# A hybrid decoder block on one core: the split weights of even and odd channel tiles are laid half a block and 128 bytes apart

## The chip, the cores and the metric

One of the eight cores of a Trainium2 chip runs the whole layer. The metric is the device time in microseconds of one execution; the kernel before took 1539.01 us (median of 3 runs, 1537.67 to 1539.15).

## The reference

The input is 256 tokens of width 2048; 16 learned meta tokens are put in front, which makes 272. All numbers are float32.

```
xn   = rms(h, n1);  proj = xn @ w_in                # 2048 x 10704
z_rwkv, z_fox, z_gate = split(proj)
y_a  = rwkv7(lerp of z_rwkv with the token before)  # 16 heads of 64, recurrence over tokens
y_b  = fox(z_fox)                                   # 16 heads, causal softmax with forget gates
merged = sigmoid(z_gate_a) * (y_a @ w_a) + sigmoid(z_gate_b) * (y_b @ w_b)
h    = h + merged @ w_o
gate, up = split(rms(h, n2) @ w_gate_up)            # 2048 x 2 x 5632
out  = h + (silu(gate) * up) @ w_down               # 5632 x 2048; the meta tokens are dropped
```

## The kernel before

Every large product is done with split operands. A float32 weight block `raw` of 128 partitions by 1024 columns is loaded by a DMA from SyncE's queue; ScalarE rounds it into `wh` (type float32r, the high part), VectorE subtracts and leaves `wl` (the low part). This is `wload` (L304). Activations are held as such pairs too: `xhl` (the normed input), `hts` (the FFN's input), `yas` and `ybs` (the branches) have the shape [128, channel tile, 2, 272], so high and low part of one channel tile lie side by side and one channel tile comes 2 x 272 = 544 columns (2176 bytes) after the other. A product is then high x high + high x low + low x high, all float32r, added up in PSUM.

A weight block of 1024 columns is `kb` channel tiles of `cols` columns each: two of 512 in the FFN (`gt`, `up`), w_o and w_down; four of 256 in the products of w_in and in the branches (`br`). In the kernel before they lie one behind the other, so the channel tiles of a block start 2048 or 1024 bytes apart.

`cm_jobs` (L432) makes products with the weights stationary and the tokens moving. For each of the block's `nm` output tiles of 128 columns and each channel tile it either calls `mm2` (L418: one matmul of 512 columns, high weights against both parts of 256 tokens, then one of 256 columns with the low weights) or `mm3` (L346 to 349: three matmuls of n columns: high weights and high tokens, high weights and low tokens, low weights and high tokens). n is 272 for k, v of RWKV and k, v of fox, 258 for RWKV's r, 256 for the branches; `mm2` serves the gates `zg`, fox's q (`f` with 512 columns), `gt` and `up`. Each matmul is preceded by a load of its 128x128 stationary tile (LDWEIGHTS), which the profile lists as PEld and which overlaps the matmul ahead of it.

`tm_jobs` (L1286) serves w_o (`wo`) and w_down (`dn`): there the activations (`mgh`, `mgl`, `ach`, `acl`; step 1024 bytes from one channel tile to the next) are stationary and the weights move, 512 columns in two rows of 256. `wload` is called with `gap=True` for it and puts each row of 256 columns behind 16 free ones, in steps of 272. Its three matmuls are L1304 (high activations, high weights), L1305 (low, high), L1306 (high, low).

The order of the work on TensorE is written out by hand (`manual_schedule`): `run` loads a block, does the multiplications of the block before, and so on; between matmuls `slot` (L386) lets in the small steps of the RWKV recurrence and of the attention when their due time has come. The other engines are put in order by a planner. Weights have four buffers each for `raw`, `wh` and `wl` in a pool at the low end of SBUF, ahead of `xhl` and `hts`. In this layout all weight buffers begin 128 bytes past a multiple of 256, and so do `xhl` and `hts`; `yas`, `ybs`, `mgh`, `mgl`, `ach`, `acl` begin 224 bytes past one.

In the RWKV recurrence `XT` (a transposed 32x32 block for each of 8 chunks and 2 heads) and `QT` are two tiles of 128 x 8 x 32. XT is written by VectorE, 16 matmuls read one half of its rows, ScalarE copies their result into the other half of the rows of QT (L962), and 16 matmuls read that.

Of the kernel before, what the change touches and what calls it, by code (L numbers as in the profile page):

```python
# [9 lines left out]
F32 = mybir.dt.float32  # L10
# [8 lines left out]
P = 128  # L19
D = 2048  # L20
NMETA = 16

T = 256
L = NMETA + T
# [10 lines left out]
KT = D // P  # L35
# [17 lines left out]
EB = 8  # L53
GATEB = 3
PSM = 4
WCOLS = 4 * L

LANES = 112
BETWEEN = 2
# [41 lines left out]
def hybrid_block(ctx, tc, A, out, dbg=None):  # L101
    nc = tc.nc
# [31 lines left out]
    for h in range(2):  # L134
        rows = slice(h * HD, (h + 1) * HD)
# [50 lines left out]
    rw = rw_pool.__enter__()  # L186
# [114 lines left out]
        nc.tensor.matmul(pz, zw, zw, start=True, stop=True)  # L301


    def wload(parts, n, between=None, gap=False):  # L304

        raw = wp.tile([P, 1024], F32, tag="raw", name="raw", bufs=RAWB)
        wh = wp.tile([P, WCOLS], F32R, tag="wh", name="wh", bufs=WB)
        wl = wp.tile([P, WCOLS], F32R, tag="wl", name="wl", bufs=WB)  # L310
        if gap:

            (_, _, shape, ((_, src),)), = parts
            nc.sync.dma_start(raw.rearrange("p (k c) -> p k c", c=shape[1]), src)
            rr = raw.rearrange("p (r c) -> p r c", c=T)
            th, tl = (t.rearrange("p (r c) -> p r c", c=L)[:, :, NMETA:] for t in (wh, wl))
            nc.scalar.activation(th, rr, AF.Copy)  # L317
            nc.vector.tensor_tensor(tl, rr, th.bitcast(F32), op=ALU.subtract)  # L318
            return [(th, tl)]
        res = []  # L320
        for prow, c0, shape, srcs in parts:
            size = 1
            for d in shape:
                size *= d
            names = " ".join(f"d{i}" for i in range(len(shape)))
            kw = {f"d{i}": d for i, d in enumerate(shape)}

            def v(t):
                return t[:prow, c0:c0 + size].rearrange(f"p ({names}) -> p {names}", **kw)

            for sel, src in srcs:
                nc.sync.dma_start(v(raw)[sel], src)
            if between is not None:
                between(len(res))
            cs_ = slice(c0, c0 + size)
            nc.scalar.activation(wh[:prow, cs_], raw[:prow, cs_], AF.Copy)  # L336
            nc.vector.tensor_tensor(wl[:prow, cs_], raw[:prow, cs_], wh[:prow, cs_].bitcast(F32), op=ALU.subtract)  # L337
            res.append((v(wh), v(wl)))
        return res

    ALL = slice(None)

    def kblock(ap):
        return ap.rearrange("(k p) c -> p k c", p=P)

    def mm3(ps, wh, wl, ah, al, first, last):  # L346
        nc.tensor.matmul(ps, wh, ah, start=first, stop=False)  # L347
        nc.tensor.matmul(ps, wh, al, start=False, stop=False)  # L348
        nc.tensor.matmul(ps, wl, ah, start=False, stop=last)  # L349
# [58 lines left out]
    def run(jobs):  # L408
        for load, mul in jobs:
            w = load()  # L410
            finish_job()
            pending.append(lambda w=w, mul=mul: mul(w))
# [6 lines left out]
    def mm2(ps, wh, wl, act, first, last):  # L419

        if last:
            nc.tensor.matmul(ps[:, :T], wl, act[:, 0, :], start=False, stop=False)
        nc.tensor.matmul(ps.rearrange("p (a t) -> p a t", a=2), wh, act, start=first, stop=last)  # L423
        if not last:
            nc.tensor.matmul(ps[:, :T], wl, act[:, 0, :], start=False, stop=False)  # L425
# [3 lines left out]
        nc.scalar.activation(dst, ps[:, :T], AF.Copy)  # L429
        nc.vector.tensor_tensor(dst, dst, ps[:, T:], op=ALU.add)  # L430

    def cm_jobs(wap, nk, act, n0, n, post, alloc=main_ps, name="cm", two=True):  # L432


        box = []
        cols = wap.shape[1]
        nm, kb = cols // P, 1024 // cols

        def mk(q):
            def load():  # L440
                return wload([(P, 0, [kb, cols], [((ALL,), kblock(wap[q * kb * P:(q + 1) * kb * P, :]))])], 1024)

            def mul(w):
                (wh, wl), = w
                if q == 0:
                    box.extend(alloc(f"{name}_{m}") for m in range(nm))
                for m in range(nm):
                    ms = slice(m * P, (m + 1) * P)
                    for k in range(kb):
                        kt = q * kb + k  # L450
                        a = act[:, kt, :, n0:n0 + n]
                        if n == T and two:
                            mm2(box[m], wh[:, k, ms], wl[:, k, ms], a, kt == 0, kt == nk - 1)
                        else:
                            mm3(box[m][:, :n], wh[:, k, ms], wl[:, k, ms], a[:, 0], a[:, 1], kt == 0, kt == nk - 1)
                        slot(3 * n / 2.4)
                if q == nk // kb - 1:
                    post(box)
            return load, mul
        return [mk(q) for q in range(nk // kb)]  # L460
# [47 lines left out]
    def lora_jobs():  # L508
        box = []

        def mk(q):
            def load():
                raw = raw0 if q == 0 else wp.tile([P, 1024], F32, tag="raw", name="raw", bufs=RAWB)
                wh = wp.tile([P, WCOLS], F32R, tag="wh", name="wh", bufs=WB)
                wl = wp.tile([P, WCOLS], F32R, tag="wl", name="wl", bufs=WB)
                if q > 0:
# [197 lines left out]
    def rwkv_bg(g, box):  # L714
        kr, vr, rr, sg_, ag, gg = (box[n] for n in ("k", "v", "r", "sig", "aa", "gg"))
        rr = rr[:, :, :T]
# [55 lines left out]
        parts = [et(f"{n}{g}").bitcast(F32R)[:, :, :T] for n in ("rkh", "rkl")]  # L772
# [98 lines left out]
        for s_ in range(31):  # L871
            n, w = s_ // 3 + 1, 31 - s_
# [6 lines left out]
        for j in range(3):  # L879
            n = 11 if j < 2 else 10  # L880
# [68 lines left out]
        meta_steps = step(-1, S, BK0, SV0, NK0, X0, None)  # L949

        XT = rw.tile([P, 8, 32], F32, tag="xt", name=f"XT{g}", bufs=1)
        QT = rw.tile([P, 8, 32], F32, tag="qt", name=f"QT{g}", bufs=1)
        nc.vector.transpose(XT, X[:, :, 0:32])
        next(meta_steps)
        yield Y_XT, ("chain", 2)
        ps = aux_ps(f"QT{g}")
        up, dn = (lambda h: slice(h * HD, h * HD + 32)), (lambda h: slice(h * HD + 32, h * HD + HD))
# [36 lines left out]
        for cc in range(2):  # L994
            for h in range(2):
                dst = yg[hb(h)].rearrange("p m (e f t) -> p m e f t", f=2, t=HD)[:, :, :, cc, :]
                src = ps[hb(cc), :].rearrange("p (m e h t) -> p m e h t", m=2, e=2, h=2)[:, :, :, h, :]
# [189 lines left out]
    gt = None  # L1187
# [36 lines left out]
    gt = gt_pool.__enter__()  # L1224
# [55 lines left out]
    hts = hp.tile([P, KT, 2, L], F32R, tag="hts", name="hts")  # L1280
# [4 lines left out]
    def tm_jobs(wap, nk, ah, al, post, name):  # L1285

        box = []

        def mk(q):
            def load():  # L1290
                return wload([(P, 0, [2, 512], [((ALL,), kblock(wap[q * 256:(q + 1) * 256, :]))])], 1024, gap=True)

            def mul(w):
                (wh, wl), = w
                if q == 0:
                    box.extend(main_ps(f"{name}_{t}") for t in range(2))
                end = q == nk // 2 - 1
                for k, t in ((0, 0), (1, 0), (0, 1), (1, 1)):
                    kt = q * 2 + k
                    ts_ = slice(t * P, (t + 1) * P)  # L1300
                    first, last = kt == 0, kt == nk - 1
                    o = box[t].rearrange("p (a c) -> p a c", a=2)
                    hi, lo_ = wh[:, 2 * k:2 * k + 2], wl[:, 2 * k:2 * k + 2]
                    nc.tensor.matmul(o, ah[:, kt, ts_], hi, start=first, stop=False)  # L1304
                    nc.tensor.matmul(o, al[:, kt, ts_], hi, start=False, stop=False)  # L1305
                    nc.tensor.matmul(o, ah[:, kt, ts_], lo_, start=False, stop=last)  # L1306
                    if end and k == 1:
                        post(t, box[t])
            return load, mul
        return [mk(q) for q in range(nk // 2)]  # L1310
# [41 lines left out]
    wgu = A["w_gate_up"][0]  # L1352
    for j in range(DFF // 512):
        gs = [hp.tile([P, T], F32, tag="ga", name=f"ga{j}{m}", bufs=8) for m in range(4)]

        def post_gate(pss, gs=gs):
            for g, ps in zip(gs, pss):
                halves(g, ps)
                nc.vector.tensor_tensor(g, g, rsb2, op=ALU.mult)
                nc.scalar.activation(g, g, AF.Silu)  # L1360

        def post_up(pss, gs=gs, j=j):
            for m, (g, ps) in enumerate(zip(gs, pss)):
                ub = hp.tile([P, T], F32, tag="ub", name=f"ub{j}{m}", bufs=2)
                halves(ub, ps)
                nc.vector.tensor_tensor(ub, ub, rsb2, op=ALU.mult)
                nc.vector.tensor_tensor(ub, ub, g, op=ALU.mult)
                split(ach[:, 4 * j + m, :], acl[:, 4 * j + m, :], ub)
        run(cm_jobs(wgu[:, j * 512:(j + 1) * 512], KT, hts, NMETA, T, post_gate, name=f"gt{j}"))
        run(cm_jobs(wgu[:, DFF + j * 512:DFF + (j + 1) * 512], KT, hts, NMETA, T, post_up, alloc=aux_ps, name=f"up{j}"))  # L1370
    wdn = A["w_down"][0]
    for j in range(4):
# [70 lines left out]
```

## Time and profile before

| | |
|---|---|
| median of 3 runs | 1539.01 us (1537.67 to 1539.15) |
| the profiled execution | 1540.85 us |
| its span in the trace | 1539.1 us |
| PE busy | 1529.6 us (99%), 10113 matmul records |
| PE weight loads busy | 1352.5 us (88%) |
| VectorE, ScalarE, GpSimd busy | 1030.4, 778.2, 106.8 us |
| DMA | 283.32 MB, mean 184 GB/s |

The span runs from the first to the last instruction of the profiled execution. The length that is recorded for one matmul is longer than the time to the start of the next, as matmuls overlap; what the engine needs for one is seen in the distance of the starts. By time, the products of w_in with the recurrence and the attention run to about 613 us, the branches to 705, w_o to 797, `gt` and `up` to 1291 and w_down to the end.

### The profile page before, as it was taken

Reading aid. Unit: us, or ns where it says so; the run is one execution under the profiler, and the core shown is the slowest. Engines: PE = TensorE matmul, PEld = TensorE weight load, DVE = VectorE, ACT = ScalarE, POOL = GpSimd, SP = SyncE. Lnnn points to the kernel's source line nnn. Section 1 sums busy time; section 2 is a strip of 40 time slices with the busy share of each in tenths; the row PEclk is TensorE's granted clock in tenths of the full one; section 3 lists DMA queues with packets and bytes.
Section 4 is the critical chain, followed back from the end, with each engine's and each line's share of the span. In section 5 each row is a group of like instructions: output and inputs, shape, how many; then the busy total and the mean of one; then the engine's idle time right before and its main releaser. Section 6 shows DMA issues by size and latency. Waiting matters only on the chain.

```text
span 1539.1 us, 25987 instructions
## 1 busy us (share of the span) xinstructions
PE 1529.6 (99%) x10113; PEld 1352.5 (88%) x10113; DVE 1030.4 (67%) x1859; ACT 778.2 (51%) x1174; POOL 106.8 (7%) x186
## 2 busy tenths in 40 slices
PE   9999999999999999999999999999999999999998
PEld 9999899989989888998888888888888888888887
DVE  7887698688788857876565566666556666444443
ACT  7654465475465445554455455445445544333332
POOL 2111203302202000000000000000000000000000
PEclk9999999999999999999999999999999999999999
DMA  8566546546645757777566666666666665566663
GB/s 269 163 171 185 148 134 188 163 119 188 175 125 154 212 155 218 230 226 240 181 180 185 192 185 186 191 192 182 189 191 191 182 190 189 191 204 204 189 203 104
DMA packets 211483, 283.32 MB, mean 184 GB/s; under 512 B 23888, under 2 KB 128352, under 8 KB 211360
## 3 DMA queue, kind: packets, MB, share of 16 engines
q1 hardware_dynamic: 206752, 277.53, 60.7%
q10 hardware_dynamic: 4608, 4.13, 0.8%
q8 instruction: 79, 1.29, 0.3%
q14 instruction: 44, 0.36, 0.1%
HBM read 274.43 MB, written 7.19 MB: 183 GB/s over the span
## 4 chain that ended last, share of the span: by engine, by line
PE 95%; DVE 2%; ACT 1%; DMA 1%; SPq 1%; issue 1%; DVEq 0%; ACTq 0%
PE up L423 11%; PE gt L423 10%; PE zg L423 8%; PE dn L1306 5%; PE dn L1305 5%; PE dn L1304 5%; PE up L425 5%; PE gt L425 5%; PE zg L425 4%; PE f L347 2%; PE f L349 2%; PE f L348 2%; PE br L347 2%; PE f L423 2%; PE br L348 2%; PE br L349 2%
## 5 line engine op out<-in xcount | busy, mean ns | idle before, releaser
L337 DVE TENSOR_TENSOR wl<-raw,wh 128x1024 fp32r<-128x1024 f32 (+1 forms) x376 | 456.7, 1216 | 264.0 <-ACT wh L336 263.4
L336 ACT ACTIVATE wh<-raw 128x1024 fp32r<-128x1024 f32 (+1 forms) x376 | 393.9, 1049 | 424.8 <-PE up L423 117.5
L318 DVE TENSOR_TENSOR wl<-raw,wh 128x1024 fp32r<-128x1024 f32 x120 | 147.0, 1225 | 162.8 <-ACT wh L317 162.7
L423 PE MATMUL gt<-hts,wh 128*128 128x512 f32 x704 | 245.0, 394 | 0.0
L423 PE MATMUL up<-hts,wh 128*128 128x512 f32 x704 | 244.9, 394 | 0.0
L317 ACT ACTIVATE wh<-raw 128x1024 fp32r<-128x1024 f32 x120 | 127.0, 1058 | 194.4 <-PE dn L1305 141.5
L425 PE MATMUL gt<-hts,wl 128*128 128x256 f32 x660 | 186.2, 282 | 0.0
L425 PE MATMUL up<-hts,wl 128*128 128x256 f32 x660 | 186.0, 282 | 0.0
L423 PE MATMUL zg<-xhl,wh 128*128 128x512 f32 x512 | 182.4, 401 | 0.0
L423 PEld LDWEIGHTS up<-hts,wh 128*128 128x128 f32 x704 | 130.1, 188 | 26.5
L423 PEld LDWEIGHTS gt<-hts,wh 128*128 128x128 f32 x704 | 130.1, 188 | 26.5
L1305 PE MATMUL dn<-wh,acl 128*128 128x512 f32 x352 | 138.7, 394 | 0.0
L1306 PE MATMUL dn<-wl,ach 128*128 128x512 f32 x352 | 138.3, 393 | 0.0
L1304 PE MATMUL dn<-wh,ach 128*128 128x512 f32 x352 | 138.1, 392 | 0.0
L425 PE MATMUL zg<-xhl,wl 128*128 128x256 f32 x480 | 135.0, 281 | 0.0
L425 PEld LDWEIGHTS up<-hts,wl 128*128 128x128 f32 x660 | 124.7, 189 | 1.8
L425 PEld LDWEIGHTS gt<-hts,wl 128*128 128x128 f32 x660 | 124.7, 189 | 1.8
L423 PEld LDWEIGHTS zg<-xhl,wh 128*128 128x128 f32 x512 | 94.3, 188 | 19.4 <-issue 0.7
L425 PEld LDWEIGHTS zg<-xhl,wl 128*128 128x128 f32 x480 | 90.6, 189 | 1.2
L1304 PEld LDWEIGHTS dn<-wh,ach 128*128 128x128 f32 x352 | 66.0, 188 | 15.7
L1305 PEld LDWEIGHTS dn<-wh,acl 128*128 128x128 f32 x352 | 66.1, 188 | 15.4
L1306 PEld LDWEIGHTS dn<-wl,ach 128*128 128x128 f32 x352 | 66.1, 188 | 14.7
(464 smaller groups left out, 2937.9 us busy)
## 6 DMA issues: line engine op xcount, KB each, us to landing
raw<-in_w_gate_up_dram SPq DMA_DIRECT2D x176, 512.0 KB, 3.7
raw<-in_w_in_dram SPq DMA_DIRECT2D x160, 512.0 KB, 4.1
raw<-in_w_down_dram SPq DMA_DIRECT2D x88, 512.0 KB, 4.8
raw<-in_w_o_dram SPq DMA_DIRECT2D x32, 512.0 KB, 4.1
raw<-in_w_branch_a_dram SPq DMA_DIRECT2D x16, 512.0 KB, 4.6
raw<-in_w_branch_b_dram SPq DMA_DIRECT2D x16, 512.0 KB, 4.7
zgd<-zg ACTq DMA_DIRECT2D x30, 128.0 KB, 1.7
gate<-zgd SPq DMA_DIRECT2D x15, 256.0 KB, 6.0
```

The source lines that it names most:

```text
L317: nc.scalar.activation(th, rr, AF.Copy)
L318: nc.vector.tensor_tensor(tl, rr, th.bitcast(F32), op=ALU.subtract)
L336: nc.scalar.activation(wh[:prow, cs_], raw[:prow, cs_], AF.Copy)
L337: nc.vector.tensor_tensor(wl[:prow, cs_], raw[:prow, cs_], wh[:prow, cs_].bitcast(F32), op=ALU.subtract)
L347: nc.tensor.matmul(ps, wh, ah, start=first, stop=False)
L348: nc.tensor.matmul(ps, wh, al, start=False, stop=False)
L349: nc.tensor.matmul(ps, wl, ah, start=False, stop=last)
L423: nc.tensor.matmul(ps.rearrange("p (a t) -> p a t", a=2), wh, act, start=first, stop=last)
L425: nc.tensor.matmul(ps[:, :T], wl, act[:, 0, :], start=False, stop=False)
L1304: nc.tensor.matmul(o, ah[:, kt, ts_], hi, start=first, stop=False)
L1305: nc.tensor.matmul(o, al[:, kt, ts_], hi, start=False, stop=False)
L1306: nc.tensor.matmul(o, ah[:, kt, ts_], lo_, start=False, stop=last)
```

## The change

The weight buffers grow from 1088 to 1152 columns (`WCOLS`). `wload` gets the layout as `lay`, a pair of first columns, for the high and for the low weights. For the products of `cm_jobs` the even channel tiles of a block go into one half and the odd ones into another that begins 544 columns (512 + 32, so 2176 bytes) later; the first columns come from the table `LAY`, by the number of moving columns, `LAYG` for `gt`. For `tm_jobs` the rows of 256 keep their step of 272, and the second channel tile begins 576 columns (2304 bytes) after the first, where it was 544. Matmuls, their order and their shapes stay; the slices of `wh` and `wl` follow the layout. To make room, `QT` becomes the same tile as `XT`, and the scratch for DMA descriptors at the start of SBUF shrinks from 2048 to 1024 bytes for each partition.

```diff
-WCOLS = 4 * L
+WCOLS = 1152
+LAY = {L: (32, 32), T + 2: (32, 32), T: (32, 32), 2 * T: (0, 0)}
+LAYG = (0, 24)
+LAYT = (16, 16)
...
-    def wload(parts, n, between=None, gap=False):
+    def wload(parts, n, between=None, lay=None, rows=False):
...
-        if gap:
+        if lay is not None:
             (_, _, shape, ((_, src),)), = parts
-            nc.sync.dma_start(raw.rearrange("p (k c) -> p k c", c=shape[1]), src)
-            rr = raw.rearrange("p (r c) -> p r c", c=T)
-            th, tl = (t.rearrange("p (r c) -> p r c", c=L)[:, :, NMETA:] for t in (wh, wl))
+            k, c = shape
+            nc.sync.dma_start(raw.rearrange("p (k c) -> p k c", c=c), src)
+            if rows:
+                rr = raw.rearrange("p (k r c) -> p k r c", k=2, r=2)
+                th, tl = (t.rearrange("p (k e) -> p k e", k=2)[:, :, s - NMETA:s + NMETA + 2 * T]
+                          .rearrange("p k (r c) -> p k r c", c=L)[:, :, :, NMETA:] for t, s in zip((wh, wl), lay))
+            else:
+                rr = raw.rearrange("p (j q c) -> p q j c", q=2, c=c)
+                th, tl = (t[:, s:s + 1088].rearrange("p (q e) -> p q e", q=2)[:, :, :512]
+                          .rearrange("p q (j c) -> p q j c", c=c) for t, s in zip((wh, wl), lay))
             nc.scalar.activation(th, rr, AF.Copy)
             nc.vector.tensor_tensor(tl, rr, th.bitcast(F32), op=ALU.subtract)
...
+                             lay=lay or LAY[2 * T if n == T and two else n])
...
-                            mm2(box[m], wh[:, k, ms], wl[:, k, ms], a, kt == 0, kt == nk - 1)
+                            mm2(box[m], wh[:, k % 2, k // 2, ms], wl[:, k % 2, k // 2, ms], a, kt == 0, kt == nk - 1)
...
-        QT = rw.tile([P, 8, 32], F32, tag="qt", name=f"QT{g}", bufs=1)
+        QT = XT
...
-                    hi, lo_ = wh[:, 2 * k:2 * k + 2], wl[:, 2 * k:2 * k + 2]
+                    hi, lo_ = wh[:, k], wl[:, k]
...
-        run(cm_jobs(wgu[:, j * 512:(j + 1) * 512], KT, hts, NMETA, T, post_gate, name=f"gt{j}"))
+        run(cm_jobs(wgu[:, j * 512:(j + 1) * 512], KT, hts, NMETA, T, post_gate, name=f"gt{j}", lay=LAYG))
...
-    nc = _bacc.Bacc("TRN2", target_bir_lowering=False, num_devices=1, dynamic_dma_scratch_size=2048)
+    nc = _bacc.Bacc("TRN2", target_bir_lowering=False, num_devices=1, dynamic_dma_scratch_size=1024)
```

## Rows read from the trace of the kernel before

**Rows 1.** The page: busy time, granted clock in 40 slices, chain by engine.
```profile
PE 1529.6 (99%) x10113; PEld 1352.5 (88%) x10113; DVE 1030.4 (67%) x1859; ACT 778.2 (51%) x1174; POOL 106.8 (7%) x186
...
PEclk9999999999999999999999999999999999999999
...
PE 95%; DVE 2%; ACT 1%; DMA 1%; SPq 1%; issue 1%; DVEq 0%; ACTq 0%
```

**Rows 2.** Waits of PE, longest total first: us in total, times, longest.
```profile
PE X L373 <- ACT QT L962: 2.0, 4, 1.5
PE warmup L301 <- DVE yb L298: 1.1, 1, 1.1
```

**Rows 3.** Timeline of PE in w_down: start us, recorded length us; L1304 alone.
```profile
1399.86 0.39 PE L1304 MATMUL dn<-wh,ach 128*128 128x512 f32 x1
...
1400.55 0.39 PE L1304 MATMUL dn<-wh,ach 128*128 128x512 f32 x1
...
1401.24 0.39 PE L1304 MATMUL dn<-wh,ach 128*128 128x512 f32 x1
...
1401.94 0.39 PE L1304 MATMUL dn<-wh,ach 128*128 128x512 f32 x1
...
1404.02 0.39 PE L1304 MATMUL dn<-wh,ach 128*128 128x512 f32 x1
```

**Rows 4.** Lines of w_down, 1300 to 1534 us: recorded length min/median/max ns.
```profile
L1304 PE MATMUL dn<-wh,ach x338: 392/392/393, 1300.0 to 1533.7; 128*128 128x512 f32 x169
...
L1305 PE MATMUL dn<-wh,acl x338: 392/394/396, 1300.2 to 1533.9; 128*128 128x512 f32 x169
...
L1306 PE MATMUL dn<-wl,ach x338: 392/393/394, 1299.8 to 1533.4; 128*128 128x512 f32 x169
```

**Rows 5.** Lines of the branches, 618 to 700 us, the same columns.
```profile
L347 PE MATMUL br<-yas,wh x116: 282/284/285, 618.0 to 699.0; 128*128 128x256 f32 x116
...
L348 PE MATMUL br<-yas,wh x117: 279/279/282, 617.8 to 699.1; 128*128 128x256 f32 x117
```

**Rows 6.** Lines of the wide product v, 390 to 412 us.
```profile
L348 PE MATMUL v<-xhl,wh x32: 284/288/291, 397.2 to 411.5; 128*128 128x272 f32 x32
...
L349 PE MATMUL v<-xhl,wl x32: 285/288/291, 397.3 to 411.7; 128*128 128x272 f32 x32
```

**Rows 7.** L423 in the FFN, 850 to 1280 us, and gt's two around 900.4.
```profile
L423 PE MATMUL gt<-hts,wh x621: 388/393/399, 849.7 to 1268.4; 128*128 128x512 f32 x156
L423 PE MATMUL up<-hts,wh x609: 388/393/399, 865.4 to 1279.8; 128*128 128x512 f32 x153
...
L423 PE MATMUL gt<-hts,wh x2: 393/394/396, 900.1 to 900.4; 128*128 128x512 f32 x2
```

**Rows 8.** Timeline of PE, L347 in the wide products: first and last of eight.
```profile
394.42 0.28 PE L347 MATMUL k<-xhl,wh 128*128 128x272 f32 x1
...
397.05 0.29 PE L347 MATMUL v<-xhl,wh 128*128 128x272 f32 x1
```

**Rows 9.** The page's groups of the splits: busy us, mean ns; idle before.
```profile
L337 DVE TENSOR_TENSOR wl<-raw,wh 128x1024 fp32r<-128x1024 f32 (+1 forms) x376 | 456.7, 1216 | 264.0 <-ACT wh L336 263.4
L336 ACT ACTIVATE wh<-raw 128x1024 fp32r<-128x1024 f32 (+1 forms) x376 | 393.9, 1049 | 424.8 <-PE up L423 117.5
L318 DVE TENSOR_TENSOR wl<-raw,wh 128x1024 fp32r<-128x1024 f32 x120 | 147.0, 1225 | 162.8 <-ACT wh L317 162.7
...
L317 ACT ACTIVATE wh<-raw 128x1024 fp32r<-128x1024 f32 x120 | 127.0, 1058 | 194.4 <-PE dn L1305 141.5
```

**Rows 10.** Line L1304 in w_o, 700 to 810 us.
```profile
L1304 PE MATMUL wo<-wh,mgh x128: 388/392/402, 705.0 to 796.1; 128*128 128x512 f32 x128
```

More of the change, by code (lines that the diff above doesn't have):

```diff
@@ L430, in halves, with cm_jobs @@
         nc.vector.tensor_tensor(dst, dst, ps[:, T:], op=ALU.add)
-    def cm_jobs(wap, nk, act, n0, n, post, alloc=main_ps, name="cm", two=True):
+    def cm_jobs(wap, nk, act, n0, n, post, alloc=main_ps, name="cm", two=True, lay=None):
         box = []
@@ L440, in load @@
             def load():
-                return wload([(P, 0, [kb, cols], [((ALL,), kblock(wap[q * kb * P:(q + 1) * kb * P, :]))])], 1024)
+                return wload([(P, 0, [kb, cols], [((ALL,), kblock(wap[q * kb * P:(q + 1) * kb * P, :]))])], 1024,
+                             lay=lay or LAY[2 * T if n == T and two else n])
             def mul(w):
@@ L452, in mul @@
                         if n == T and two:
-                            mm2(box[m], wh[:, k, ms], wl[:, k, ms], a, kt == 0, kt == nk - 1)
+                            mm2(box[m], wh[:, k % 2, k // 2, ms], wl[:, k % 2, k // 2, ms], a, kt == 0, kt == nk - 1)
                         else:
-                            mm3(box[m][:, :n], wh[:, k, ms], wl[:, k, ms], a[:, 0], a[:, 1], kt == 0, kt == nk - 1)
+                            mm3(box[m][:, :n], wh[:, k % 2, k // 2, ms], wl[:, k % 2, k // 2, ms], a[:, 0], a[:, 1],
+                                kt == 0, kt == nk - 1)
                         slot(3 * n / 2.4)
@@ L1290, in load @@
             def load():
-                return wload([(P, 0, [2, 512], [((ALL,), kblock(wap[q * 256:(q + 1) * 256, :]))])], 1024, gap=True)
+                return wload([(P, 0, [2, 512], [((ALL,), kblock(wap[q * 256:(q + 1) * 256, :]))])], 1024,
+                             lay=LAYT, rows=True)
             def mul(w):
```

## The prediction
> **What bounds the kernel.** I read the page first. [...] The view of waits is read next: the longest total that PE waited for any one producer is 2.0 us, for an activation that writes QT [rows 2]. So weights, DMAs, ScalarE and VectorE are all in time, and the end is set by how long 9,450 matmuls take one after another. Then I asked whether that length is what it must be. [...] L1305 runs from 392 to 396 ns with a median of 394, which is half at 392 and half at 396 [rows 4]; in the branch stage L347 has 282 or 285 and L348 has 279 or 282 [rows 5]; in the wide products v has 284 to 291 in L348 and 285 to 291 in L349 [rows 6]; gt and up have 393 as median of L423 and a second kind some 3 ns longer, which the two neighbours of one window show as 393 and 396 [rows 7].
>
> **What tells the two kinds apart.** In order of time they alternate with the channel tile. I averaged the trace's start times from the first matmul of one channel tile to that of the next, over all undisturbed tiles of a parity (even tile, odd tile, ns): k 379.2 and 372.9, v 380.6 and 372.7, fox's 272-wide ones 377.5 and 374.1, r 366.6 and 356.5, branch 360.0 and 353.3, gt and up 349.2 and 351.0, zg 349.7 and 350.7, w_down 690.0 and 696.7, w_o 687.4 and 700.3. Rows print starts to 10 ns; [rows 3] shows w_down's 0.69 and 0.70, and [rows 8] eight starts of the wide product k whose first and last are seven tiles and 2.63 us apart, 376 ns each, which is the mean of its two kinds.
> The code gives what alternates. Activations of one channel tile and the next lie 2 x 272 floats = 2176 bytes apart, eight and a half times 256. Weights of consecutive tiles lie 1024 or 2048 bytes apart. So the distance from the weights to the activations, modulo 256, jumps by 128 with each tile. All weight buffers start 128 bytes past a multiple of 256, as do xhl and hts; yas, ybs, mgh and ach 224 past one. That gives these distances (first weight byte minus first byte of the high activations, modulo 256; even, odd tile): 272 wide 0, 128; r (258) 200, 72; branch 96, 224; pairs of 512 and 256 columns 192, 64. In w_o and w_down the weights are the moving operand and move by 2176 bytes while the activations stand still: activations minus weights 32, 160. In every kind one of the two is slow, and the fast ones are 128, 72, 224, 192, 32.
>
> **The change part by part.**
> *Even and odd tiles 544 columns apart.* 544 floats are 2176 bytes, the step of the activations, so the distance is the same for both parities. With first columns (32, 32) it is 128 for 272 wide, 72 for r, 224 for branch; with (0, 0) it is 192 for the pairs: each time the fast one. For w_o and w_down the halves are 576 columns, 2304 bytes = 9 x 256, apart, and both stand at 32, the fast one too. That assumes that the first byte of a buffer stays where it is modulo 256: the scratch shrinks by 1024 bytes, four times 256, and a buffer is 4608 bytes, eighteen times 256, so it does.
> *The sum,* each kind with half the difference of its two tiles, as half of them change (the counts are loop counts): k 128 x 3.2 = 0.41, v 128 x 4.0 = 0.51, fox 256 x 1.7 = 0.44, r 128 x 5.0 = 0.64, branch 256 x 3.4 = 0.86, gt and up 1408 x 0.9 = 1.27, zg and fox's q 640 x 0.5 = 0.32, w_down 352 x 3.4 = 1.18, w_o 128 x 6.5 = 0.83; together 6.5 us. All of it is on PE, which waits for nothing, so all of it is on the path.
> *gt's low weights 24 columns (96 bytes) further.* Its distance for the low load becomes 192 + 96 = 32 modulo 256. No row of before has that with activations moving; the nearest is w_down's fast tile at 32, at 230 ns a matmul against 230.8 for L423 at 192, and the branch's slow one at 96, 5 ns over its fast one in L347's starts. Bounds over 704 pairs: 0.6 us less, 3.5 us more. I take 0.3 less, by the row with the same distance.
> *The last load of a tile* belongs to the next tile, where the distance is now flipped by 128. Before, both cases are present at that place: L425 takes 117.7 and 118.4, k's L349 125.0 and 126.2 ns to the next start, no more than 1.2 ns either way. I take nothing; 128-byte steps in the two ends are worth at most 1 us over 1,000 tiles.
> *Split with cut rows.* The activation and the subtraction now always write in pieces. w_down's already do: 1058 against 1049 ns and 1225 against 1216 ns [rows 9]. That is 9 ns, 376 times, on ScalarE and VectorE, 3.4 us each. ScalarE waits for PE to free a buffer before it splits, so four buffers of some 2.8 us of matmuls hide it. If that cover were gone it would cost 18 ns a load, 6.8 us.
> *QT on top of XT.* The copy into QT waits for the matmuls that read XT anyway, since their sums are what it copies, and it writes the other rows. PE's 2.0 us of waiting for it [rows 2] stays; nothing, or at most a copy's length four times, about 1 us. The smaller scratch moves addresses only: nothing. DMAs and matmuls keep count, order and size.
>
> The profiled execution took 1540.9 us, 1.8 more than its span of 1539.1; the runs' median is 1539.0. 6.8 us of 1540.9 is 0.44%, so on the median 1539.0 - 6.8 = 1532.2 us.
>
> [...]
>
> **The rivals.**
> *A, the stall is shared, not owned.* w_o has two rhythms: in one the fast tile's matmuls start 230, 231, 229 ns apart and the slow one's 230, 235, 232, in the other 226, 228, 229 and 237, 232, 235; both sum to 1387. So a slow tile may lend time that a fast one gives back, and with all tiles alike the mean of today may remain; L1304's 388 to 402 ns in w_o [rows 10] shows how far it swings. Or the moving operand's own place decides, and then only w_down and w_o gain, 2.0 us. Against it: branch and w_down hold one rhythm throughout [rows 4, 5]. [...]
> *B, the stalls feed each other and vanish.* With no slow tile ahead each kind may settle at its shortest rhythm: w_o's 683 instead of 693.5 for w_o's and w_down's 480 triples is 5.0 us, 226 for 231 in 2,048 pairs 10.2 us, the other kinds 3.2 us as above: 18.4 us, 1520.6. For it: w_o does reach 226 for dozens of matmuls. Against: only next to 237.
> *C, slower: both parities on the slow side.* The distance is fixed by where buffers start. If a buffer's start moves by 128 against its activations, each first column picks the slow distance and the sum turns round: 1539.0 + 6.5 = 1545.5. It decides from an odd multiple of 128 bytes in what is allocated ahead of the weights; the sizes above speak against it. gt's 3.5 us above would come on top or, alone, halve the gain.
> *D, the pieces are late.* PE would wait for wl; 6.8 us would eat the gain whole, 1539. Against it: PE never waits for a split in the FFN [rows 2].
>
> **How the numbers follow.** Forecast 0.60, with its own range 1529 to 1536 (half a nanosecond a matmul, 9,450 x 0.5 = 4.7 us, about the middle). A and D together 0.18, B 0.15, C 0.07. A difference of 0.2% is 3.1 us and about what a measurement of this kernel can tell from none. Faster: 0.58 of the forecast and all of B, and a little of A where gains elsewhere come on top, 0.75. Same: 0.18. Slower: 0.07. The range is from 1523, most of B's way, to 1538.5, which holds half of A and leaves C out.
>
> **What would show it.** After the change the recorded lengths of L1304 to L1306 should be of one kind, 392 to 393 ns with no 396; L347 and L348 in the branch 282 and 279 only; v's L348 near 287; L423 393 with no 396. Starts of w_down's triples should all be 0.69 apart. Stages: w_down 1.2 us shorter, the FFN's first half 1.6, the rest before it 4. PE's waits should not grow. The forecast is wrong if the two kinds are still there, if they are gone and the mean stays, or if a wait for wl appears.

## The result and the profile after

The kernel after takes 1543.95 us (median of 7 runs, 1542.94 to 1545.81) against 1538.76 us before (7 runs, 1537.22 to 1539.15): 1.0036 times as long, interval 1.0026 to 1.0046. The forecast was 1532.2 us. The profiled execution took 1544.48 us, its span 1542.8 us, 3.7 more than before.

The page of the kernel after, the rows that answer [rows 1]:

```profile
PE 1534.5 (99%) x10113; PEld 1353.1 (88%) x10113; DVE 1032.0 (67%) x1859; ACT 778.5 (50%) x1174; POOL 104.7 (7%) x186
...
PEclk9999999999999999999999999999999999999999
...
PE 95%; DVE 2%; DMA 1%; ACT 1%; SPq 1%; issue 0%; DVEq 0%; ACTq 0%
```

PE's waits after (us in total, times, longest), the rows that answer [rows 2]:

```profile
PE X L386 <- ACT XT L978: 1.5, 2, 1.4
PE warmup L306 <- DVE yb L303: 1.1, 1, 1.1
```

The same number of matmuls (10113) at the same granted clock (0.999 of full speed in both traces), the same share of the chain (95%), no longer wait: PE alone is 4.9 us longer busy. So the time is again in the distance from one start to the next.

w_down after, timeline of its first matmul (start us, recorded length us), the rows that answer [rows 3]:

```profile
1400.10 0.40 PE L1321 MATMUL dn<-wh,ach 128*128 128x512 f32 x1
1400.81 0.39 PE L1321 MATMUL dn<-wh,ach 128*128 128x512 f32 x1
...
1404.31 0.40 PE L1321 MATMUL dn<-wh,ach 128*128 128x512 f32 x1
```

First and last are six triples apart: 4.21 us where [rows 3] show 4.16. Averaged over the stage a triple takes 700.0 ns; before it took 690.0 in even tiles and 696.7 in odd ones. The tiles are not all alike: by the start times a round of four (698, 698, 705, 699 ns) repeats to the end of the column blocks, though every tile has the same distance modulo 256.

The lines of w_down from 1300 to 1534 us (recorded length min/median/max ns), for [rows 4]:

```profile
L1321 PE MATMUL dn<-wh,ach x335: 392/395/398, 1300.0 to 1533.8; 128*128 128x512 f32 x168
L1322 PE MATMUL dn<-wh,acl x334: 392/396/398, 1300.2 to 1533.3; 128*128 128x512 f32 x167
L1323 PE MATMUL dn<-wl,ach x335: 392/396/398, 1299.8 to 1533.6; 128*128 128x512 f32 x168
```

The prediction wanted 392 to 393 and no 396. The middles are now 395, 396 and 396, and every tile of the round is slower than both kinds of before. (A *rhythm* is from here on the pattern of distances between starts that repeats from tile to tile.)

The same columns for the branches (for [rows 5]), v (for [rows 6]), the FFN's first products (for [rows 7]) and w_o (for [rows 10]):

```profile
L360 PE MATMUL br<-yas,wh x114: 280/280/284, 617.8 to 697.5; 128*128 128x256 f32 x114
L361 PE MATMUL br<-yas,wh x114: 279/282/284, 617.9 to 697.6; 128*128 128x256 f32 x114
...
L361 PE MATMUL v<-xhl,wh x32: 284/288/291, 395.6 to 409.9; 128*128 128x272 f32 x32
L362 PE MATMUL v<-xhl,wl x32: 286/287/288, 395.8 to 410.0; 128*128 128x272 f32 x32
...
L436 PE MATMUL gt<-hts,wh x619: 388/395/397, 849.8 to 1269.5; 128*128 128x512 f32 x155
L436 PE MATMUL up<-hts,wh x606: 390/397/402, 864.8 to 1279.9; 128*128 128x512 f32 x152
...
L1321 PE MATMUL wo<-wh,mgh x128: 391/396/401, 703.6 to 795.4; 128*128 128x512 f32 x128
```

In the branches even and odd tiles now average the same (354.4 ns, before 360.0 and 353.3), in a round of three tiles (358, 353, 352); in the wide products they came nearer to each other (372.6 to 375.1, before 372.7 to 380.6). Only these became shorter. In up two kinds of tile are still there, further apart than before: 348.2 and 358.3 ns, where it was 349.2 and 351.0. The first matmuls of four tiles in a row, in up's first column block (512 output columns) and in its third:

```profile
828.69 0.39 PE L436 MATMUL up<-hts,wh 128*128 128x512 f32 x1
...
829.03 0.40 PE L436 MATMUL up<-hts,wh 128*128 128x512 f32 x1
...
829.39 0.39 PE L436 MATMUL up<-hts,wh 128*128 128x512 f32 x1
...
829.74 0.40 PE L436 MATMUL up<-hts,wh 128*128 128x512 f32 x1
```

```profile
912.63 0.39 PE L436 MATMUL up<-hts,wh 128*128 128x512 f32 x1
...
912.98 0.40 PE L436 MATMUL up<-hts,wh 128*128 128x512 f32 x1
...
913.34 0.39 PE L436 MATMUL up<-hts,wh 128*128 128x512 f32 x1
...
913.68 0.40 PE L436 MATMUL up<-hts,wh 128*128 128x512 f32 x1
```

Recorded lengths of 0.39 and 0.40 alternate. In the first stretch 0.40 are the even tiles, in the second the odd ones: counted through the whole stage from the start times, the slow tile (358 ns) is the even one in the first of up's eleven column blocks and the odd one in the other ten. All these tiles have one distance modulo 256, and the column blocks go through the same weight buffers, so the slow kind does not belong to a distance here.

The timeline of k for [rows 8]:

```profile
392.52 0.28 PE L360 MATMUL k<-xhl,wh 128*128 128x272 f32 x1
...
395.13 0.29 PE L360 MATMUL k<-xhl,wh 128*128 128x272 f32 x1
```

Seven tiles take 2.61 us here, 2.63 in [rows 8].

The splits after (busy us, mean ns; idle before), for [rows 9]:

```profile
L331 DVE TENSOR_TENSOR wl<-raw,wh 128x1024 fp32r<-128x1024 f32 x488 | 598.0, 1226 | 428.8 <-ACT wh L330 428.0
L330 ACT ACTIVATE wh<-raw 128x1024 fp32r<-128x1024 f32 x488 | 516.6, 1059 | 619.9 <-PE dn L1322 143.6
```

They cost 10 ns more each, as foreseen, and PE has no wait for them among its longest.

Where the 3.7 us are: I added up, from the trace's start times, the time from each matmul to the next by product. "Memory alone" is the first experiment below, in which no distance changes; it shows which rows of this table can be trusted.

| us, after minus before | predicted | after | memory alone |
|---|---|---|---|
| w_down | -1.18 | +2.34 | 0.00 |
| w_o | -0.83 | +0.72 | -0.02 |
| up | -0.64 | +2.23 | 0.00 |
| gt | -0.94 | -0.20 | +0.02 |
| zg and fox's q | -0.32 | +1.41 | -0.02 |
| branches | -0.86 | -0.55 | 0.00 |
| wide k, v, fox | -1.36 | -2.00 | -1.37 |
| r | -0.64 | -0.56 | -0.45 |
| lo (low-rank products, first 30 us) | 0 | +0.49 | +1.36 |

In the kernels below each of the first six rows is within 0.04 us of before wherever its product has the layout of before. k, v, r and lo run beside the recurrence and change by up to 1.4 us between two kernels with the same layout ("memory alone"); for them the period of undisturbed tiles is the better reading.

### The profile page after: what moved, and what is told of

It reads as the page before. It is cut to its first block, busy times and chain, and to the rows that moved or that the text cites. A ratio compares the mean times of both kernels' runs of the same rounds, so it can differ in the third digit from the quotient of the medians.

```text
span 1542.8 us, 25987 instructions
## 1 busy us (share of the span) xinstructions
PE 1534.5 (99%) x10113; PEld 1353.1 (88%) x10113; DVE 1032.0 (67%) x1859; ACT 778.5 (50%) x1174; POOL 104.7 (7%) x186
## 4 chain that ended last, share of the span: by engine, by line
PE 95%; DVE 2%; DMA 1%; ACT 1%; SPq 1%; issue 0%; DVEq 0%; ACTq 0%
PE up L436 11%; PE gt L436 10%; PE zg L436 8%; PE dn L1322 5%; PE dn L1321 5%; PE dn L1323 5%; PE up L438 5%; PE gt L438 5%; PE zg L438 4%; PE f L360 2%; PE f L362 2%; PE f L436 2%; PE f L361 2%; PE br L360 2%; PE br L361 2%; PE br L362 2%
## 5 line engine op out<-in xcount | busy, mean ns | idle before, releaser
L331 DVE TENSOR_TENSOR wl<-raw,wh 128x1024 fp32r<-128x1024 f32 x488 | 598.0, 1226 | 428.8 <-ACT wh L330 428.0
L330 ACT ACTIVATE wh<-raw 128x1024 fp32r<-128x1024 f32 x488 | 516.6, 1059 | 619.9 <-PE dn L1322 143.6
L436 PE MATMUL up<-hts,wh 128*128 128x512 f32 x704 | 247.2, 396 | 0.0
L436 PE MATMUL gt<-hts,wh 128*128 128x512 f32 x704 | 244.9, 395 | 0.0
L438 PE MATMUL up<-hts,wl 128*128 128x256 f32 x660 | 186.8, 283 | 0.0
L438 PE MATMUL gt<-hts,wl 128*128 128x256 f32 x660 | 185.3, 281 | 0.0
L436 PE MATMUL zg<-xhl,wh 128*128 128x512 f32 x512 | 183.5, 402 | 0.0
L436 PEld LDWEIGHTS up<-hts,wh 128*128 128x128 f32 x704 | 130.0, 188 | 27.3
L436 PEld LDWEIGHTS gt<-hts,wh 128*128 128x128 f32 x704 | 129.9, 188 | 26.5
L438 PE MATMUL zg<-xhl,wl 128*128 128x256 f32 x480 | 135.6, 283 | 0.0
L438 PEld LDWEIGHTS up<-hts,wl 128*128 128x128 f32 x660 | 125.2, 190 | 2.0
L438 PEld LDWEIGHTS gt<-hts,wl 128*128 128x128 f32 x660 | 124.9, 189 | 1.8
L436 PEld LDWEIGHTS zg<-xhl,wh 128*128 128x128 f32 x512 | 94.4, 188 | 19.8 <-issue 0.7
L438 PEld LDWEIGHTS zg<-xhl,wl 128*128 128x128 f32 x480 | 90.9, 189 | 1.2
L360 PE MATMUL f<-xhl,wh 128*128 128x272 f32 x256 | 76.3, 298 | 0.0
L362 PE MATMUL f<-xhl,wl 128*128 128x272 f32 x256 | 73.7, 288 | 0.0
```

## The experiments

A *place* is where the weights of a block begin, given by their two first columns (high, low); a *pair* is a product with matmuls of 512 and 256 columns, a *triple* the three matmuls of a tile of the others. Theory *Places*: the ns of a matmul are set inside PE, by where the two operands lie, and the changed pairs, w_down and w_o were given worse places. Its rivals: the memory moves (buffer starts, QT on XT) did it; other engines' and DMA's writes meet PE's reads. Distances are first weight byte minus first byte of the activations modulo 256 from here on (expectations that speak of 32 and 160 for w_o and w_down count the other way round, as the prediction does; the change's place is 224 in this count, before it was 224 and 96; the 176 of two expectations is already in this count).

**Which part.** Three kernels. The first is the kernel before with the change's memory alone:

```diff
-WCOLS = 4 * L
+WCOLS = 1152
...
-dynamic_dma_scratch_size=2048
+dynamic_dma_scratch_size=1024
-        QT = rw.tile([P, 8, 32], F32, tag="qt", name=f"QT{g}", bufs=1)
+        QT = XT
```

> The kernel before with 1152-column buffers, QT in XT's tile and the smaller scratch, and no distance changed. Theory S: as before, 1538 to 1539.5. Rival M: 1542 to 1544.

Measured 1539.17 us, 0.9998 of before (0.999 to 1.0007). Buffer starts and QT are out.

The second is the kernel after with the halves of w_o and w_down 544 apart again:

```diff
-th, tl = (t.rearrange("p (k e) -> p k e", k=2)[...]
+th, tl = (t[:, :1088].rearrange("p (k e) -> p k e", k=2)[...]
```

> The changed kernel, with the halves of w_o's and w_down's weights back at 544 columns apart (channel tiles alternate between the distances 32 and 160 again). Theory S (a run of matmuls settles into a rhythm that depends on the whole sequence of distances, and one constant distance can settle at a slow one): the two stages get back the 3.1 us that they lost between the profiles (w_down 246.2 to 243.8, w_o 90.2 to 89.5), the whole about 1541. Rival M (the loss comes from larger buffers, the shared tile, the smaller scratch or the cut rows of the splits): stays at 1544.

Measured 1540.62 us, 1.0007 (0.9998 to 1.0016). w_down is 243.84 us and w_o 89.43, both within 0.04 of before; up keeps its +2.23.

The third also takes the pairs back (halves 512 apart, first columns (0, 0) for `gt` too), so that only the three-matmul products are changed:

```diff
-th, tl = (t[:, s:s + 1088].rearrange("p (q e) -> p q e", q=2)[...]
+th, tl = (t[:, s:s + (1088 if s else 1024)].rearrange("p (q e) -> p q e", q=2)[...]
-LAYG = (0, 24)
+LAYG = (0, 0)
```

> The changed kernel with the new distances in the products of three matmuls alone (k, v, r, fox's 272-wide ones, branches); pairs and moving weights alternate as before. Theory S: keeps their gain of 3.1 us and loses the 6.8 us that up, zg, w_o and w_down cost: 1535.5 to 1536.5, w_down 243.8 us, up 246.4 us. Rival M: 1544 still, the loss spread over all stages.

Measured 1537.66 us, 0.9989 (0.998 to 0.9998), 1.2 us above the range expected; its runs spread from 1535.66 to 1539.91. Everything lost is back; the branches keep their -0.56. By the first six rows each part of the change acts on its own product alone. The line of w_down in the second kernel (recorded length min/median/max ns):

```profile
L1321 PE MATMUL dn<-wh,ach x352: 392/392/395, 1290.7 to 1534.1; 128*128 128x512 f32 x176
```

392 is back by the halves alone, with all else as in the kernel after.

**Does anyone else take part?** The kernel after, in which w_down loads and splits four blocks and then uses them over and over (84 of its 88 loads and splits are left out):

```diff
...
+                if nk > KT and i >= WB:
+                    return KEPT[i % WB]
...
```

> The changed kernel, but w_down multiplies with its first four weight blocks over and over: the other 84 blocks are neither loaded nor split (left out of the computation), so no DMA, ScalarE or VectorE writes run beside its matmuls. Theory T (the rhythm is between PE's own weight loads and its stream): w_down's triples stay at 700 ns, stage 246 us. Rival W (the writes of the splits and DMAs hold the run at its slow rhythm): under 695 ns, towards 690.

Measured 1544.41 us in one run; w_down +2.34 us against before, as in the kernel after, and 700.0 ns a triple. Busy time by engine in a stretch of w_down (stretch, its length, then PE, PEld, DVE, ACT, POOL, granted clock, DMA share, GB/s), first the kernel after, then this one:

```profile
1310.00:1530.00 220.00, 220.00 (x944) 176.70 (x943) 100.58 (x85) 82.81 (x79) 0.00 (x0) 1.00 0.62 189
```

```profile
1310.00:1530.00 220.00, 220.00 (x945) 176.69 (x944) 4.16 (x6) 0.00 (x0) 0.00 (x0) 1.00 0.02 8
```

179 us of VectorE's and ScalarE's work and 181 GB/s go, and PE makes 945 matmul records instead of 944. So in w_down the 2.34 us are lost without the others' work too. (The pairs were not run without traffic.)

**Where are the good places?** In this kernel each weight block has its own first columns, 0 to 56 in steps of 8 for high and for low (columns of w_o and w_down up to 48), so that one run tries dozens of places for each kind (56 can be read for gt and up):

```diff
...
+    i = SEEN[kind] = SEEN.get(kind, -1) + 1
+    return 8 * (i % 8), 8 * (i // 8 % 8)
...
```

> The changed kernel with first columns that go through an 8 by 8 grid of 32-byte steps for high and low weights, another pair for each weight block (moving weights 7 by 7; zg and fox's q with halves 512 apart, so that distances alternate). Read block by block from the starts. Theory S: the time to the next channel tile varies over the grid by some per cent, with pairs of first columns under 349 ns and triples of w_down under 690. Rival F (one floor that no place goes under: 349 for a pair, 690 for a triple): only equal or slower points. Rival N (place is nothing, the run's rhythm is chance): no pattern, the same place gives different times in different blocks.

Measured 1539.01 us in one run. Averages by place over undisturbed pairs go from 343.3 to 356.5 ns in gt and up. The change's place, (0, 0), with both distances 192, has 352.9, the fifth slowest of 56; (32, 0), high at 64 and low at 192, has 343.3. There is no smooth rule in the table. In gt and up a place follows the same other place each time, so the map does not separate a place from what ran before it. Starts of L444, first at (0, 0), then at (32, 0), from the same run:

```profile
974.27 0.40 PE L444 MATMUL gt<-hts,wh 128*128 128x512 f32 x1
...
976.75 0.39 PE L444 MATMUL gt<-hts,wh 128*128 128x512 f32 x1
...
985.18 0.40 PE L444 MATMUL gt<-hts,wh 128*128 128x512 f32 x1
...
986.90 0.39 PE L444 MATMUL gt<-hts,wh 128*128 128x512 f32 x1
```

Seven pairs in 2.48 us (354 ns) at (0, 0), five in 1.72 (344) at (32, 0).

**Is it the next tile's load?** While the last matmul of a tile streams, the high weights of the *next* tile are loaded: in the kernel after, up's L438 and the 0.19 us load for the next tile's L436 are both recorded from 1189.85 us, and that L436 itself from 1189.96. The halves 544 apart keep a tile's own distance, but put this load 128 further: at (0, 0) the low load meets the stream at 192, the next high load at 64. With the high weights 32 columns (128 bytes) further it meets it at 192 too. The second kernel above with that, w_o and w_down as before:

```diff
-LAY = {..., 2 * T: (0, 0)}
+LAY = {..., 2 * T: (32, 0)}
-LAYG = (0, 24)
+LAYG = (32, 0)
```

> The kernel of e2 with the halves of all pairs (zg, fox's q, gt, up) 544 columns apart and first columns (32, 0), so that each weight load, the one for the next channel tile too, meets the activations that stream beside it at the same distance, 192. Theory T (what counts is the distance of the load in flight to the stream of its own time; the change kept the low load at 192 and put the next tile's high load at 64): pairs take 343.3 ns as in the map's blocks with this place, gt and up 237.3 us each (before 246.7), zg 5 us less, the whole about 1523 to 1525. Rival U (the map's blocks gained because their neighbours had other places, and a run with one place locks as w_down did): pairs at 350 or above, the whole at 1537 or more.

("237.3 us each" is a slip: 704 pairs of 343.3 ns are 241.7 us. zg, expected 5 us shorter, gained 1.5; with both, the expected 1523 to 1525 was missed.) Measured 1528.08 us, 0.9928 (0.9916 to 0.9941). up is 242.15 us, 6.48 less than in the kernel after, for 128 bytes in the high weights; gt is 242.94, zg 182.78. Lines of up in this kernel:

```profile
L436 PE MATMUL up<-hts,wh x704: 388/388/398, 816.6 to 1278.6; 128*128 128x512 f32 x176
```

The median is 388 where it was 397. That the pair likes both loads at 192 fits the place, but the tiles of the kernel before that had both at 192, the even ones, took 349.2, not 343.6, next to neighbours with both at 64. So a tile's time hangs on its neighbours as well. A second map asked whether there is a hollow around (32, 0):

```diff
...
+    if kind == "ffn":
+        return 24 + 2 * (i % 9), (56, 58, 60, 62, 0, 2, 4, 6, 8)[i // 9 % 9]
...
```

> A second map: gt and up in 8-byte steps around (32, 0), branches over the low columns not seen yet, the wide products over the 8 by 8 grid alone, w_o and w_down with halves 544 apart over the 8 by 8 grid, zg at (32, 0). Theory T: a hollow around (32, 0), 343 ns at its floor, rising to 350 within some 32 bytes; zg at 343. Rival V (only multiples of 32 or 64 bytes count): steps, not a slope.

Measured 1538.32 us in one run, and there is none: (30, 6) averages 356.6 ns, and (30, 4) and (32, 6), two columns off, 347. (32, 0) itself came twice, each time behind a block at (30, 0); the first time that block is the last one of gt's column block:

```profile
L448 PE MATMUL up<-hts,wh x7: 392/399/399, 906.4 to 908.5; 128*128 128x512 f32 x7
...
L448 PE MATMUL up<-hts,wh x6: 388/388/388, 1133.6 to 1135.3; 128*128 128x512 f32 x6
```

The same place in the same kernel averages 355.5 ns a pair in one block and 343.8 in the other.

**The best places of the maps**, put together:

```diff
+LAY = {L: (32, 56), T + 2: (48, 0), T: (56, 16), 2 * T: (32, 0)}
+LAYG = (32, 0)
+LAYT = (8, 16)
...
```

> As e5, and the best places of the map for the rest: wide products (32, 56), r (48, 0), branches (56, 16), w_o and w_down high 8, low 16 with halves 576 apart. Theory T: wide triples 371 ns (before 376), branch 350 (before 357), w_down 690 to 691 (before 693), so some 5 us less than e5: 1518 to 1520. Rival U: these kinds are no better than in e5, with w_down at 700 if it locks.

Measured 1524.67 us, 0.9907 (0.9892 to 0.9922): 3.4 us less than with the pairs alone at (32, 0), where some 5 were expected. Branches take 350.0 ns a tile, w_down 690.0 and w_o 690.1 a triple on average (685 and 695 alternate), k and v 370.6.

With L: (40, 0) and T + 2: (8, 8) beside it:

> As e6, with the wide products at (40, 0) and r at (8, 8). Theory T with the maps: wide triples 370.0 ns in place of 370.6 to 373.0, r 356.5 in place of 359: about 0.8 us less than e6, 1524. Rival U (the map's blocks don't transfer to a run): no better than e6, or worse.

Measured 1524.35 us, 0.9899 (0.9882 to 0.9915): no more than the one before, within what can be told. A finer map for w_o and w_down (4-column steps) in the first of these two kernels found one place, (4, 4), that held 680 in all four of its triples; the next best come to 686 or 687 within their block:

> As e6, with w_o's and w_down's weight blocks at another place each, in 16-byte steps, halves 576 apart. Theory T: most places lock at 700 or wander between 690 and 700, a few go under 690. Rival F (690 is a floor): none under 690 in steady run.

Measured 1526.66 us in one run.

**Is w_down's loss a matter of place alone?** The kernel after with nothing but the first columns of w_o and w_down moved from (16, 16) to (4, 4); even and odd tiles keep one distance, 176 instead of 224:

```diff
-LAYT = (16, 16)
+LAYT = (4, 4)
...
```

> The changed kernel with LAYT (4, 4) in place of (16, 16): the distance of w_o's and w_down's loads goes from a constant 32 to a constant 176, nothing else. Theory T: 700 to 680 ns a triple, 9.6 us less than the changed kernel, 1534 to 1535. Rival S: no change, 1544.

Measured 1535.90 us, 0.9983 of before (0.9974 to 0.9992). w_down falls from 246.16 to 239.13 us, the other products of the table's first six rows stay as in the kernel after to 0.1 us. w_o is 90.21 us, still slow, which the expectation did not have. Its lines in w_down, nearly all of one length:

```profile
L1322 PE MATMUL dn<-wh,ach x352: 389/389/391, 1291.6 to 1530.3; 128*128 128x512 f32 x176
L1323 PE MATMUL dn<-wh,acl x352: 389/389/389, 1291.8 to 1530.5; 128*128 128x512 f32 x176
L1324 PE MATMUL dn<-wl,ach x352: 389/389/389, 1292.0 to 1530.7; 128*128 128x512 f32 x176
```

(4, 4) in the kernel with the best places:

> As e9, with w_o's and w_down's weights at first columns (4, 4), halves 576 apart: one distance, 176, for all their loads, the place that ran at 680 ns a triple in the third map. Theory T: 680 in every triple, w_down 239.2 us (before 243.8), w_o 87.6, the whole 4.8 us under e9: 1519.5. Rival S (a run with one distance locks at 700, whatever it is): w_down 246 us, the whole 1531.

Measured 1521.32 us, 0.9884 (0.9871 to 0.9898): w_down 239.15 us, 680.0 a triple; w_o again 90.21 (87.6 expected), 699.9 a triple. 680 and 700 at one place, in one kernel, each held for a whole stage.

**Does the run remember how it began?** The first block of each of w_o's four column blocks got a place of its own, the other seven of each column block stayed at (4, 4):

```diff
-                             lay=LAYT, rows=True)
+                             lay=LAYT if nk > KT or q else {"wo0": (44, 0), "wo1": (36, 0), "wo2": (12, 0), "wo3": (8, 16)}[name], rows=True)
```

> As e11, but the first weight block of each of w_o's four column blocks lies at another place, (44, 0), (36, 0), (12, 0) and (8, 16); the seven after it at (4, 4) as in e11. Theory H (two rhythms exist at one place, and the run keeps the one that it came in with): in at least one of the four the later blocks run at 680 ns a triple. Rival X (w_o's own addresses hold it at 700): 700 in all later blocks of all four.

Measured 1522.14 us in one run. The first column block holds 680 (226, 226, 227), the other three hold 700 (233, 234, 233) to their end. Lines of w_o, 702.5 to 720 us and 726 to 743 us, all at (4, 4):

```profile
L1322 PE MATMUL wo<-wh,mgh x26: 389/389/390, 702.7 to 719.7; 128*128 128x512 f32 x26
...
L1322 PE MATMUL wo<-wh,mgh x24: 395/395/396, 726.2 to 742.3; 128*128 128x512 f32 x24
```

The same seven blocks of the first column block in the kernel before this one, where only the first block lies elsewhere (702.5 to 720 us):

```profile
L1322 PE MATMUL wo<-wh,mgh x25: 395/395/396, 702.7 to 719.5; 128*128 128x512 f32 x25
```

So (4, 4) has two rhythms in w_o, 680 and 700, and in this column block the first block alone decided which. Does the change's own place have a fast one that it missed? The same with the kernel after and w_down, four other first blocks:

```diff
+                             lay={"dn0": (8, 12), "dn1": (0, 4), "dn2": (44, 0), "dn3": (48, 12)}.get(name, LAYT) if q == 0 else LAYT, rows=True)
```

> The changed kernel with its own place for w_down, (16, 16), distance 32, in all blocks but the first of each of its four column blocks, which lies at (8, 12), (0, 4), (44, 0), (48, 12). Theory H (as in e14: at one place there is a slow and a fast rhythm, and the change came in on the slow one): in at least one column block the following 21 blocks run under 690 ns a triple. Rival Y (at the distance 32 there is only the slow rhythm): 700 in all four.

Measured 1547.22 us in one run; w_down's four column blocks all stay at 700. In four entries the change's place showed its slow rhythm only; that it has no other is not shown.

**The best version.** The best places, (4, 4) for w_down, (8, 16) for w_o:

```diff
+                             lay=LAYT if nk > KT else (8, 16), rows=True)
```

> As e11, with w_o's weights at (8, 16) again and w_down's at (4, 4): w_o 88.95 us in place of 90.21, w_down 239.15 as there, the whole 1.3 us under e11: about 1520.

Measured 1520.52 us, 0.9872 of before (0.9855 to 0.9888): w_down 239.15 us, w_o 88.95, up 242.14, branches 89.60. Its page:

```profile
PE 1510.1 (99%) x10113; PEld 1342.4 (88%) x10113; DVE 1029.5 (68%) x1859; ACT 778.1 (51%) x1174; POOL 107.6 (7%) x186
```

10,113 matmuls again, in 24.4 us less PE time than in the kernel after. Between this and the kernel with w_o at (4, 4) only w_o's place differs, yet gt, which comes next, differs too. Its first column block at (32, 0), first with w_o at (4, 4), then in this version:

```profile
L437 PE MATMUL gt<-hts,wh x53: 387/388/388, 792.6 to 811.1; 128*128 128x512 f32 x53
```

```profile
L437 PE MATMUL gt<-hts,wh x50: 392/399/400, 792.9 to 810.9; 128*128 128x512 f32 x50
```

343.4 and 356.6 ns a pair, at one place with one layout of gt: the pairs have two rhythms too. Nor does a rhythm always last: in the kernel that first had the pairs at (32, 0), gt's first column block left the slow one after 24 of its 64 tiles.

## Why the prediction was wrong

- *What bounds the kernel, and that places cost time: right.* No wait, clock or other engine explains the loss: the longest total that PE waited for one producer is 1.5 us where it was 2.0, the granted clock 0.999 in both, VectorE 1.6 and ScalarE 0.3 us longer busy. In w_down the loss stayed the same without traffic, and 48 bytes (12 columns) in where its weights begin are worth 7.03 us.
- *"What tells the two kinds apart" failed.* It gave each kind to a distance (one slow, one fast). With one distance for all tiles up still has two kinds, 348.2 and 358.3 ns, and which parity is slow differs between its column blocks. The prediction's own sign, that the two kinds are still there, came true.
- *"The sum", built on it, failed.* It took the shorter period of an alternating pair as a property of its distance and gave it to all tiles. For w_down the term was -1.18 us and measured +2.34. The distance that stood beside 690 in alternation runs at 700.0 alone: slower than both tiles before and than their mean of 693.3. So 690 was the period of a tile in that alternating sequence, not of its distance. The kernel after with (4, 4) shows that a constant distance as such is no fault, for it gives 680. The branches (-0.55 for -0.86) and wide tiles (mean of the two kinds down by 2 to 3 ns, forecast 3 to 4 for k and v) are the terms where reading it so came near; there too tiles run in rounds (358, 353, 352 in the branches), not at the fast tile's 353.3, so the size is in part luck. The sum's range used 9,450 matmuls, a number that no row has: the products with split weights have some 8,500 records.
- *"The last load of a tile", taken at nothing, failed too.* The 117.7 and 118.4 ns from which it was priced were both read where that load stood at its own tile's distance. Flipped by 128, it is a case that the trace before didn't have. Put back by 128 bytes, up goes from 248.63 to 242.15 us; the high weights of a pair are read in that load alone, so it is this load that was moved.
- *gt's low weights 96 bytes further* were priced at -0.3 within -0.6 to +3.5. gt lost nothing where up, without them, lost 2.23 us, but its gain was 0.20 of the 0.94 that it was to bring with the sum.
- *Split, QT, scratch: right.* The splits take 10 ns more, hidden; the memory alone is 0.9998.
- *The rivals.* A saw that a slow tile and a fast one share a sum, but gave no change, and the constant sequence was neither the mean nor the fast one. Its second half, that the moving operand's own place decides and only w_down and w_o gain, falls with up, which moved by 6.48 us with its stationary high weights. B's vanished stalls, 1520.6 us, are what the best version reaches, part by part too (pairs 9.3 us where B had 10.2, w_o and w_down 5.2 for 5.0), but at other places than the change's. C named 1545.5 us, near the result, but by moved buffer starts, and these stayed: the memory alone changes nothing.

What stays open: what makes such a rhythm (shown is only that w_down's 700.0 does not need the other engines or DMA), whether it is the distance of the two operands or each one's own place that counts (no run moved both alike), what in the entry picks one of two rhythms, and which places are good. Maps found them; no rule over distances foretold them.

## What to carry to other kernels

A period read for one tile in an alternating sequence wasn't that tile's price in a uniform one (w_down: 690.0 and 700.0 ns): price a new rhythm by a row in which it holds by itself for many matmuls, or call the sign open. Where PE is busy 99% and tiles of one shape take different times, as here 690.0 and 696.7 ns, one kernel with another layout in each block shows dozens of places in a run, and the winner must then be run as a whole stage, since how a stage is entered can decide its rhythm (680 or 700 in w_o's first column block).

## What the runs showed of the hardware

512-column float32r matmuls, each with a weight load, fell into rhythms that held for up to hundreds of matmuls, with means of 226.7 ns (680.0 a triple, w_down at (4, 4)), 230.0 (690.0, the even tiles of before) or 233.3 (700.0, the kernel after); a pair of 512 and 256 columns ran at 343.3 to 357. Triples of 272 columns (370.0 ns, by the maps) and of 256 (350.0, the branches at the best places) differ by 48 columns and 20.0 ns, or 0.417 ns a column; by that 512 columns would take 213 ns (an estimate from these two times). In the kernel after the times of the tiles repeat over two (up, 348.2 and 358.3), three (branches, 358, 353, 352) or four (w_down, 698, 698, 705, 699), though every tile has the same distances. In w_down the mean is 700.0 ns a triple with and without DMA and splits beside it. The seven blocks at (4, 4) of w_o's first column block kept the rhythm with which they began, 680 in one kernel and 700 in another.

PE's time moved with where its operands lie: w_down's 246.16 us fell to 239.13 by the place of the moving weights alone, up's 248.63 to 242.15 by that of the stationary high weights. Whether that is one read acting on the other, no run shows.
